# Attention layer in two stages: all projections by Strassen's scheme into DRAM, then scores to weighted values read back from DRAM, with the output projection in between

## The chip, the core and the metric

The kernel runs on one core of a Trainium2 chip. The metric is the device time of one execution in microseconds (us). The kernel before was run three times: median 2103.11 us, from 2101.34 to 2104.29. TensorE (PE) does matrix products and, with an identity matrix as one operand, transposes; its weight loads are listed apart (PEld). VectorE (DVE) and ScalarE (ACT) do elementwise work, GpSimd (POOL) does elementwise work and issues transfers, SyncE (SP) issues transfers. Each engine runs its own list of instructions in order.

## The reference

Two layers on x with 1024 tokens and 1024 channels, in float32. The first is a gated short convolution: a projection to 4 times 2048 columns, a causal convolution of width 3, gates, and a projection back to 1024. The second, which the change touches, is attention:

```python
h = rms_norm(x, attn_norm)
proj = h @ w_in                       # 1024 x (9*1024 + 1024)
for g, (window, dilation) in enumerate(((128, 1), (512, 4), (2048, 16))):
    q = rms_norm(proj_q[g], q_gain[g]); k = rms_norm(proj_k[g], k_gain[g])   # 16 heads of 64
    logits = q @ k.T / 8 + bias_g     # causal, every dilation-th token, 129 keys at most
    outs.append(softmax(logits) @ v);  lses.append(logsumexp(logits))
alpha = softmax(stack(lses), axis=0)  # weights of the three groups, by token and head
y = sum(alpha * outs) * silu(z)
x = x + y @ w_out
```

Of the 10240 columns of `proj`, 3072 each are q, k and v and 1024 are z.

## The kernel before

Activations lie transposed: 128 channels on the partitions, tokens along the free axis. A float32 product is made of three matmuls: each operand is split into a rounded high part (ACT) and the rest (DVE), and high times high, high times low and low times high are added up in PSUM. One such product covers 128 output rows, 128 contracted channels and 512 tokens.

There are four stages on PE.

*Conv input projections.* The first two of 16 column blocks (e) are plain; the other 14, two pairs each, go by Strassen's scheme: a pair of weight tiles of 128 columns by 1024 channels against both token halves needs seven block products of four contracted tiles, thus 7 x 4 x 3 = 84 matmuls (L398, L400, L401) where the plain scheme needs eight and 96. POOL adds and subtracts the weight halves (`mix`), ACT and DVE split them (L161, L162), ACT copies and DVE adds the products (L410). The weights of the next pair are prepared during this one.

*Conv output projection* (L544 to L546), 768 matmuls, for the two token halves one after the other. Its operand `yq` is read from DRAM and split. The result x1 goes to DRAM and, scaled and split, into `h1`.

*Attention projections with the attention in between.* The 80 weight tiles (q, k, v for each of 24 pairs of a head pair hp and a group g, z for each hp) are 80 x 48 = 3840 matmuls (L617 to L619). q and k get squared sums (L653, L654), one small matmul that adds and swaps them (L664), a reciprocal root (L76 to L80), a transpose that broadcasts it (L675), and a product (L682), which DVE does for q and POOL for k. v is scaled (L696) and transposed in two groups of four on PE (L705), z goes through silu. The attention of a unit (hp, g) is four steps for g = 0 and 1 and two for g = 2, thus 80 steps. A step has three parts: A, up to eight score matmuls (L759), then on DVE a maximum that also adds the bias (L767), on ACT an exponential (L770); B, up to eight transposes of the result (L780) and two copies out of PSUM by DVE or ACT in turn (L716); C, up to eight matmuls with the values (L791), then the copy of the sums `po`. After the third group of a head pair, `weights` works out the three groups' weights (L828 to L838) and sends them through DRAM (`fd`), from where they come back broadcast over partitions (`fb`, L844); D multiplies and adds (L853 to L856). What of the projections stands between two steps is set by a planner: a list of items with a cost each (0.645 for three matmuls), due times with `LEAD` and `LAST`, and `fill(to)`, which issues projection matmuls up to the due time; then C, B and A of earlier steps follow with high priority (lags 4 to 0). PE keeps the order that is written; on the other engines a scheduler sets it.

*Output projection.* Tiles 0 to 5 of the contraction (L941 to L943) start between the last steps; tiles 6 and 7 (L1014 to L1016) and the sums into `part` (L945, L1017) are the end. y goes through DRAM (`yd`) for tiles 0 to 5 and is split again (L907, L908).

## Time and profile before

The profiled execution took 2107.1 us, with a span of 2105.3 us; the mean granted clock of PE is 0.994 of full speed. Stage by stage (busy times are sums of the instructions in the window):

| window, us | what | length | PE busy | DVE busy | ACT busy | POOL busy |
|---|---|---|---|---|---|---|
| 101.0 to 641.0 | 28 Strassen pairs of the conv layer | 540.0 | 537.4 | 339.7 | 195.6 | 349.0 |
| 641.0 to 826.6 | conv output projection | 185.6 | 180.4 | 102.1 | 71.4 | 41.5 |
| 826.6 to 1975.0 | attention projections and attention | 1148.4 | 1131.9 | 611.9 | 476.6 | 159.6 |
| 1975.0 to 2105.3 | rest of the output projection | 130.3 | 111.3 | 60.0 | 32.8 | 15.8 |

A row of a grouped view (by line, or by form) names the line, engine, operation and tiles, then busy time, mean of one in ns, and the idle time of the engine just before, with what ended most of it. A matmul's mean is the length of its record, and records of PE overlap: the pitch, at which one follows the other, is window length over count.

### The profile page before, as it was taken

To read this page: it belongs to the slowest core of one execution; us is meant where nothing else is said; L and a number is where in the kernel's file an instruction comes from. 1 tells how busy PE (TensorE), PEld (TensorE's weight loads), DVE (VectorE), ACT (ScalarE), POOL (GpSimd) and SP (SyncE) were. 2 spreads that over 40 slices of the span, in tenths; PEclk is the share of its full clock that TensorE was granted. 3 is DMA by queue.
4 is the path that set the end of the run, shared out by engine and by line. 5 is a ranking of instruction groups with operands and counts; after the bars stand their busy time and mean duration, and the time that the engine had idled before them with its cause. 6 is when DMAs were issued, how large, how long until landed. Compare 5 with 4: busy or idle time off the path is not lost. (4 is left out here: it accounts for less than half of the span.)

```text
span 2105.3 us, 27817 instructions
## 1 busy us (share of the span) xinstructions
PE 2053.5 (98%) x10478; PEld 1653.8 (79%) x10478; DVE 1191.7 (57%) x2409; ACT 830.0 (39%) x1776; POOL 590.1 (28%) x568
## 2 busy tenths in 40 slices
PE   8999999999998999999999999999999999999897
PEld 6887788888886888877777777777777777777686
DVE  7866756666555554545644644645556546446544
ACT  6433333333333342243343444433433434443430
POOL 0466666666752222001201201102012012011020
PEclk9999999999999999999999999999999999999999
DMA  6245421122126553111211211212112112113142
GB/s 205 95 113 136 111 75 65 66 76 71 65 75 202 177 187 121 45 44 37 78 47 41 77 43 54 73 45 77 44 47 76 43 47 76 44 52 98 53 124 101
DMA packets 66071, 173.93 MB, mean 83 GB/s; under 512 B 9758, under 2 KB 10526, under 8 KB 65936
## 3 DMA queue, kind: packets, MB, share of 16 engines
q1 hardware_dynamic: 49248, 120.78, 18.0%
q0 software_dynamic: 16688, 51.37, 9.2%
q8 instruction: 82, 1.34, 0.3%
q14 instruction: 53, 0.43, 0.1%
HBM read 151.63 MB, written 28.87 MB: 86 GB/s over the span
## 5 line engine op out<-in xcount | busy, mean ns | idle before, releaser
L617 PE MATMUL pp<-h,whi 128*128 128x512 f32 x1280 | 513.6, 401 | 0.0
L619 PE MATMUL pp<-h,wlo 128*128 128x512 f32 x1280 | 499.7, 390 | 0.0
L618 PE MATMUL pp<-h,whi 128*128 128x512 f32 x1280 | 499.0, 390 | 0.0
L617 PEld LDWEIGHTS pp<-h,whi 128*128 128x128 f32 x1280 | 240.6, 188 | 67.5 <-issue 20.6
L69 DVE TENSOR_TENSOR wlo<-wraw,whi 128x1024 fp32r<-128x1024 f32 (+1 forms) x122 | 155.6, 1276 | 228.2 <-ACT whi L68 228.2
L619 PEld LDWEIGHTS pp<-h,wlo 128*128 128x128 f32 x1280 | 240.3, 188 | 51.6
L618 PEld LDWEIGHTS pp<-h,whi 128*128 128x128 f32 x1280 | 240.7, 188 | 45.4
L68 ACT ACTIVATE whi<-wraw 128x1024 fp32r<-128x1024 f32 (+1 forms) x122 | 127.4, 1044 | 307.2 <-PE pp L618 195.4
L770 ACT ACTIVATE xs<-xs,nl 128x128 f32<-128x128 f32 (+1 forms) x384 | 168.6, 440 | 110.6 <-DVE nl L767 110.4
L682 POOL TENSOR_TENSOR qk<-raw,tmp 128x512 f32<-128x512 f32 x48 | 62.5, 1303 | 415.7 <-DVE tmp L675 377.2
L398 PE MATMUL pp<-b,ws 128*128 128x512 f32 x448 | 174.8, 390 | 1.4 <-ACT f L406 1.4
L401 PE MATMUL pp<-b,ws 128*128 128x512 f32 x448 | 174.3, 389 | 0.0
L400 PE MATMUL pp<-b,ws 128*128 128x512 f32 x448 | 174.3, 389 | 0.0
L731 POOL DMA_DIRECT2D bt<-sk x48 | 26.8, 558 | 414.8 <-DVE nl L767 409.3
L654 DVE TRANSPOSE_TENSOR_REDUCE st<-tmp 128x16 f32<-128x512 f32 x96 | 67.9, 708 | 130.2 <-ACT tmp L653 130.0
L162 DVE TENSOR_TENSOR ws<-sr,ws 128x512 fp32r<-128x512 f32 x112 | 97.1, 876 | 69.6 <-ACT ws L161 67.7
L398 PE MATMUL pp<-t,ws 128*128 128x512 f32 x336 | 130.9, 390 | 1.2 <-ACT f L406 1.2
L400 PE MATMUL pp<-t,ws 128*128 128x512 f32 x336 | 130.7, 389 | 0.0
L401 PE MATMUL pp<-t,ws 128*128 128x512 f32 x336 | 130.7, 389 | 0.0
L162 DVE TENSOR_TENSOR ws<-wr,ws 128x512 fp32r<-128x512 f32 x100 | 107.1, 1074 | 39.5 <-ACT ws L161 38.4
L767 DVE CUSTOM_DVE_ANT_0 xs<-ps,bt 128x128 f32<-128x128 f32 (+1 forms) x384 | 111.9, 346 | 21.7 <-PE ps L759 21.5
L161 ACT ACTIVATE ws<-sr 128x512 fp32r<-128x512 f32 x112 | 70.2, 629 | 128.3 <-PE pp L401 85.6
(194 smaller groups left out, 3668.1 us busy)
## 6 DMA issues: line engine op xcount, KB each, us to landing
wr<-in_conv_w_in SPq DMA_DIRECT2D x128, 256.0 KB, 2.9
wraw<-in_wqk SPq DMA_DIRECT2D x48, 512.0 KB, 3.5
wraw<-in_conv_w_out SPq DMA_DIRECT2D x32, 512.0 KB, 4.2
wraw<-in_wv SPq DMA_DIRECT2D x24, 512.0 KB, 3.6
fb<-fd POOLq DMA_DIRECT2D x48, 256.0 KB, 4.3
f<-in_x SPq DMA_DIRECT2D x32, 256.0 KB, 5.3
ydc<-f POOLq DMA_DIRECT2D x32, 256.0 KB, 2.7
yr<-ydc SPq DMA_DIRECT2D x32, 256.0 KB, 4.0
```

What stands on the lines that cost most here:

```text
L68: nc.scalar.activation(hi[:, cs], raw[:, cs], AF.Copy)
L69: nc.vector.tensor_tensor(lo[:, cs], raw[:, cs], hi[:, cs].bitcast(F32), op=OP.subtract)
L161: nc.scalar.activation(t[:, 0], src, AF.Copy)
L162: nc.vector.tensor_tensor(t[:, 1], src, t[:, 0].bitcast(F32), op=OP.subtract)
L398: nc.tensor.matmul(ps, w[:, 0, ws], b[:, k, 0], start=new and k == 0, stop=False, skip_group_check=not new)
L400: nc.tensor.matmul(ps, w[:, 0, ws], b[:, k, 1], start=False, stop=False, skip_group_check=not new)
L401: nc.tensor.matmul(ps, w[:, 1, ws], b[:, k, 0], start=False, stop=end and k == 3, skip_group_check=not new)
L617: nc.tensor.matmul(ps, whi[:, ws], h1[:, kt, 0, cs], start=(kt == 0), stop=False)
L618: nc.tensor.matmul(ps, whi[:, ws], h1[:, kt, 1, cs], start=False, stop=False)
L619: nc.tensor.matmul(ps, wlo[:, ws], h1[:, kt, 0, cs], start=False, stop=(kt == KT - 1))
L767: nc.vector.tensor_tensor_reduce(out=x, in0=ps[s][:, x0:x0 + nk].rearrange("p a b -> p (a b)"), in1=u["bt"][s][:, bs], op0=OP.add, op1=OP. ...
L770: nc.scalar.activation(x, x, AF.Exp, bias=nm, scale=-1.0, accum_out=L)
```

## The change

The attention layer is cut in two.

1. *Blocks of the second layer's operand.* All tiles of the first stages come from one pool with seven slots of 16 KB (`blk`) and 12 + 3 tiles of 2 KB. The conv output projection runs in quarters of its contraction (`chunk(hf, dt, q)`); its first operand block is loaded in the last Strassen pair (`load_y(0, 0)`). While it runs, `row` makes the blocks that Strassen's scheme needs of h: B for the first token half, T1 and T2 (differences of blocks) from the second; `rest` makes T3, T4 and the last block after it, reading x1 back from DRAM.
2. *All 80 projection tiles as 40 Strassen pairs* (24 for q and k, 12 for v, 4 for z): 40 x 84 = 3360 matmuls in place of 3840. The seven products are PE work of lines L300 to L303 of the new kernel. `norm` of a pair stands two pairs later; all four products with the reciprocal root are on DVE now, with the gain in the same instruction. q and k go to DRAM (`qkd`) already in the order of their dilation, v transposed (`vd`; the transposes use one PSUM bank, `cst`), z after silu (`zd`). The statistics of the second token half and the two `spread` of them stand between the first pair's products.
3. *Then the 80 attention steps in a loop of their own*, without projections between them. A step's C stands three steps after its A, its B two (`LC`, `LB`), `weights` four, D eight (`LD`). The operands are loaded from DRAM six steps ahead, the bias three. `sp` has three PSUM banks in place of two, `opp` two in place of one; the copies of `po` are all on DVE.
4. *The output projection by rows of weights*: tiles 0 to 3 of the contraction as 16 groups of 12 matmuls, one in each of steps 49 to 64, tiles 4 and 5 as 16 groups of 6 in steps 69 to 84, tiles 6 and 7 at the end. y stays on chip (`y2`), split in D.

```diff
+        def block(tag=None):
+            return sl.tile([P, 4, 2, HALF], F32R, name=tag or "blk", tag="blk", bufs=7)
...
+            t = fp.tile([P, HALF], F32, name="f", tag="f", bufs=12)
...
+        def strassen(sources, pair, between, made):
+            w = [list(prepare(*sources[0]))[-1]]
+            made()
+            last = None
+            for n in range(len(sources)):
+                now = pair(n, w[n])
+                nxt = prepare(*sources[n + 1]) if n + 1 < len(sources) else iter(())
+                for at, (name, who) in enumerate(((1, now), (2, now), (4, last), (6, now), (5, now), (3, last), (7, now))):
+                    if who is not None:
+                        who[name]()
+                    between(n, at)
+                    got = next(nxt, None)
+                    if got is not None and len(w) == n + 1:
+                        w.append(got)
+                last = now
+            last[4]()
+            last[3]()
...
+                i = dt % 4
+                if hf == 0:
+                    if i == 0:
+                        B[dt // 4, 0] = block()
+                    parts_of(B[dt // 4, 0], i, x1, g2[:, dt:dt + 1])
+                elif dt < 4:
+                    if i == 0:
+                        T[1] = block()
+                    t = V1[i] = x1_tile(0, i)
+                    nc.vector.tensor_tensor(t, x1, t, op=OP.subtract)
+                    nc.scalar.activation(t, t, AF.Copy, scale=g2[:, i:i + 1])
+                    parts_of(T[1], i, t)
+                else:
+                    if i == 0:
+                        T[2] = xb.tile([P, 4, 2, HALF], F32R, name="xb", tag="xb")
+                    t = V1[i]
+                    nc.vector.scalar_tensor_tensor(t, x1, g2[:, dt:dt + 1], t, op0=OP.mult, op1=OP.subtract)
+                    parts_of(T[2], i, t)
...
+                if hf == 0:
+                    load_y(0, 0)
+                for dt in range(2):
+                    WO[dt, 0] = out_w(dt, 0)
+                for q in range(hf == 0, 4):
+                    load_y(hf, q)
+                for dt in range(2):
+                    WO[dt, 1] = out_w(dt, 1)
+                for q in range(4):
...
+                    if hf == 1 and dt == 2:
+                        stats(0, cst, sm)
+                    elif hf == 1 and dt == 3:
+                        spread(0, rtok, cst)
+                    elif hf == 1 and dt == 4:
+                        spread(0, ms2, cst)
...
+            units = [(hp, g) for hp in range(HP) for g in range(G)]
+            pairs = []
+            for m in range(12):
+                if m % 3 == 2:
+                    pairs.append(("z", 2 * (m // 3)))
+                pairs += [("qk",) + units[2 * m], ("qk",) + units[2 * m + 1], ("v", 2 * m)]
...
+                def norm():
+                    pst = cst.tile([P, HALF], F32, name="st", tag="st")
+                    nc.tensor.matmul(pst[:, :64], swap, u["st"].rearrange("p w c -> p (w c)"), start=True, stop=True)
...
+                    for hf in range(2):
+                        for which in range(2):
+                            raw = u[which, hf]
+                            rb = ftile()
+                            nc.vector.transpose(rb.rearrange("p (c q) -> p c q", q=32),
+                                                ri[:, which * 32 + hf * 16:which * 32 + (hf + 1) * 16, None]
+                                                .to_broadcast([P, 16, 32]))
+                            o = out_tile()
+                            nc.vector.scalar_tensor_tensor(o.rearrange("p (c s) -> p s c", c=c),
+                                                           raw.rearrange("p (s c) -> p s c", c=c),
+                                                           gain[:, g, which:which + 1],
+                                                           rb.rearrange("p (s c) -> p s c", c=c),
+                                                           op0=OP.mult, op1=OP.mult)
+                            nc.gpsimd.dma_start(qkd[hp, g, which].rearrange("p (c s) -> p c s", c=c)
...
+                def turn(col, q):
+                    hp, g = units[p[1] + col]
+                    vt = spare()[:, col * S:col * S + S]
+                    pv = cst.tile([P, 4, P], F32, name="st", tag="st")
+                    for i in range(4):
+                        nc.tensor.transpose(pv[:, i], blk(vt, g, 4 * q + i), ident)
+                    o = ftile()
+                    if q:
+                        nc.vector.tensor_copy(o, pv.rearrange("p a b -> p (a b)"))
+                    else:
+                        nc.scalar.activation(o, pv.rearrange("p a b -> p (a b)"), AF.Copy)
+                    nc.gpsimd.dma_start(vd[hp, g, q], o)
...
+                if kind == "qk":
+                    due[n + 2, 0] = [norm]
+                elif kind == "v":
+                    for i in range(4):
+                        due[n + 2, i + 1] = [lambda i=i: turn(i // 2, i % 2)]
...
+            def between(n, at):
+                if n == 0 and at == 1:
+                    stats(1, cst, sm)
+                elif n == 0 and at == 3:
+                    spread(1, rtok, cst)
+                elif n == 0 and at == 4:
+                    spread(1, ms2, cst)
+                for f in due.pop((n, at), ()):
...
+            def rest():
+                for n in (3, 4):
+                    T[n] = block()
+                    for i in range(4):
+                        kt = i + 4 * (n == 4)
+                        t = x1_tile(0, kt)
+                        if n == 3:
+                            nc.vector.scalar_tensor_tensor(t, t, ng2[:, kt:kt + 1], V1[i], op0=OP.mult, op1=OP.add)
+                        else:
+                            nc.vector.scalar_tensor_tensor(t, t, g2[:, kt:kt + 1], V1[i], op0=OP.mult, op1=OP.subtract)
+                        parts_of(T[n], i, t)
+                B[1, 1] = block()
+                for i in range(4):
+                    parts_of(B[1, 1], i, x1_tile(1, i + 4), g2[:, i + 4:i + 5])
...
+            strassen([sources(p) for p in pairs], pair, between, rest)
...
+        def loads(hp, g):
+            QK[hp, g] = [ap.tile([P, S], F32, name="qk", tag="qk", bufs=5) for _ in range(2)]
+            for i in range(2):
+                nc.sync.dma_start(QK[hp, g][i], qkd[hp, g, i])
+            VS[hp, g] = ap.tile([P, 8, P], F32, name="V", tag="V", bufs=3)
+            for q in range(2):
+                nc.sync.dma_start(VS[hp, g][:, 4 * q:4 * q + 4].rearrange("p a b -> p (a b)"), vd[hp, g, q])
...
-                if hp < 6:
-                    nc.gpsimd.dma_start(yd[hp], SZ[hp])
-                else:
-                    split_y(hp, SZ[hp])
+                y2[hp] = ap.tile([P, 2, S], F32R, name="y2", tag="y2", bufs=5)
+                nc.scalar.activation(y2[hp][:, 0], SZ[hp], AF.Copy)
+                nc.vector.tensor_tensor(y2[hp][:, 1], SZ[hp], y2[hp][:, 0].bitcast(F32), op=OP.subtract)
...
-                    steps.append(make(js, not steps))
+                    st = make(js, not steps)
+                    steps.append(dict(zip((0, LB, LC), st)))
                     if g == 2 and q == 1:
-                        steps[-1] += [lambda: None, D]
+                        steps[-1][LC + 1] = weights
...
+        def some(kts, dt, hf):
+            if dt not in part:
+                part[dt] = ap.tile([P, S], F32, name="part", tag="part", bufs=KT)
+                nc.sync.dma_start(part[dt], x1d[dt])
+            ps = pp1.tile([P, HALF], F32, name="pd", tag="pd")
+            dense(ps, kts, dt, hf, True, True)
+            nc.vector.tensor_tensor(part[dt][:, half(hf)], ps, part[dt][:, half(hf)], op=OP.add)
...
+            begins.setdefault(max(0, k - 6), []).append(lambda un=un: loads(*un))
+            begins.setdefault(max(0, k - 3), []).append(prefetch)
...
+        def put(kts, k):
+            begins.setdefault(k - 2, []).append(lambda: rows(kts))
+            for n, (dt, hf) in enumerate(tiles):
+                extra.setdefault(k + n, []).append(lambda dt=dt, hf=hf: some(kts, dt, hf))
+        put((0, 1, 2, 3), at[4, 0][0] + LD + 1)
+        put((4, 5), at[6, 0][0] + LD + 1)
+        end = len(steps) + LD
+        k = 0
+        while k < end or any(x >= k for x in extra):
...
+            for lag in (LD, LC + 1, LC, LB, 0):
+                if 0 <= k - lag < len(steps) and lag in steps[k - lag]:
+                    steps[k - lag][lag]()
+                if lag == LC:
+                    for f in extra.get(k, ()):
+                        f()
+            if k == end - 4:
+                rows((6, 7))
+            k += 1
```

Three places show how the instructions stand. PE, in the middle of the attention of one unit, before: `h` is the operand of the projections, `qk`, `xs`, `pts` and `V` are those of parts A, B and C.

```order
L617 MATMUL pp<-h_5694,whi 128x512
L618 MATMUL pp<-h_5694,whi 128x512
L619 MATMUL pp<-h_5694,wlo 128x512
L791 MATMUL po<-pts,V 64x128 x8
L780 MATMUL pt<-ident,xs 128x128 x6
L759 MATMUL ps<-qk 128x256 x4
L617 MATMUL pp<-h_5694,whi 128x512
L618 MATMUL pp<-h_5694,whi 128x512
L619 MATMUL pp<-h_5694,wlo 128x512
```

The same place now:

```order
L876 MATMUL pt<-ident,xs 128x128 x8
L855 MATMUL ps<-qk 128x128 x2
L855 MATMUL ps<-qk 128x256 x2
L887 MATMUL po<-pts,V 64x128 x8
L876 MATMUL pt<-ident,xs 128x128 x8
L855 MATMUL ps<-qk 128x256 x4
L887 MATMUL po<-pts,V 64x128 x8
L876 MATMUL pt<-ident,xs 128x128 x6
```

Between the parts of one step and those of the next there stands no matmul of 512 columns any more.

DVE, at the start of the projections of the attention layer, where the reciprocal root of the second token half (`rtok`, of `ms`) is made. Before, its first instructions:

```order
L107 TENSOR_SCALAR ms_79<-pp 128x4
L76 TENSOR_SCALAR rtok<-ms_79 128x4
L78 TENSOR_TENSOR rtt<-rtok 128x4
L79 SCALAR_TENSOR_TENSOR rtt<-rtt,ms_79 128x4
L80 SCALAR_TENSOR_TENSOR rtok<-rtt,rtok 128x4
```

Now, from the first instruction of its last three rounds on (`rtt`; `blk` is a block of h, `ws` a piece of a weight; L69 to L71 are what L78 to L80 were):

```order
L69 TENSOR_TENSOR rtt<-rtok 128x4
L520 TENSOR_TENSOR blk<-f,blk 128x512
L523 SCALAR_TENSOR_TENSOR blk<-f,attn_norm,blk 128x512
L520 TENSOR_TENSOR blk<-f,blk 128x512
L660 TENSOR_REDUCE st<-f 128x16
L70 SCALAR_TENSOR_TENSOR rtt<-rtt,ms_77 128x4
L166 TENSOR_TENSOR ws<-sr,ws 128x512
L71 SCALAR_TENSOR_TENSOR rtok<-rtt,rtok 128x4
```

Five of 512 columns stand between three small ones that were neighbours, and twelve more between the first of the chain (L99, which was L107) and L69; two more rounds without any in between end it. PE has its transposes of `rtok` (L107 of the new kernel) after the third product of the first pair.

DVE, from the weights of the groups (`fo`) to the first use of what comes back (`fb`). Before:

```order
L838 TENSOR_TENSOR fo<-f,mx 128x8x6
L654 TENSOR_REDUCE st<-tmp 128x16
L69 TENSOR_TENSOR wlo<-wraw,whi 128x1024
L654 TENSOR_REDUCE st<-tmp 128x16
L853 TENSOR_TENSOR o<-o,fb 128x512 x2
```

Now, around the place where L853, now L948, stands (`xs,nl<-ps,bt` is the maximum with the bias, part A):

```order
L863 ISA xs,nl<-ps,bt 128x256
L863 ISA nl 128x1
L948 TENSOR_TENSOR o<-o,fb 128x512 x2
L812 COPY pts<-pt 128x512
L863 ISA xs,nl<-ps,bt 128x128
```

Between `fo` (L838, now L933) and L948 there now stand, in place of the projections' three instructions, twelve such maxima, one copy of `po` and two of `pt`, all of later attention steps; behind L948 wait a copy of `pt` and the next step's maxima.

720 lines of the change are left out of this document (290 added, 430 removed).

## The prediction

> **What bounds the kernel now.** I read the page's busy line first, then windows by stage, then groups by form.
>
> ```profile
> PE 2053.5 (98%) x10478; PEld 1653.8 (79%) x10478; DVE 1191.7 (57%) x2409; ACT 830.0 (39%) x1776; POOL 590.1 (28%) x568
> ```
>
> PE is busy 98% of the span. The windows (core 0; length, then busy time and instructions of PE, PEld, DVE, ACT, POOL, then granted clock, DMA share, GB/s) say where it isn't:
>
> ```profile
> 101.00:641.00 540.00, 537.42 (x2359) 441.17 (x2358) 339.74 (x388) 195.55 (x333) 348.99 (x272) 1.00 0.29 84
> 641.00:826.60 185.60, 180.35 (x786) 147.74 (x786) 102.14 (x110) 71.42 (x97) 41.50 (x51) 0.98 0.56 183
> 826.60:1975.00 1148.40, 1131.93 (x6374) 902.49 (x6374) 611.90 (x1650) 476.60 (x1176) 159.61 (x194) 1.00 0.20 57
> 1975.00:2105.30 130.30, 111.31 (x556) 86.85 (x555) 60.02 (x133) 32.84 (x82) 15.78 (x22) 0.93 0.33 106
> ...
> 300.00:400.00 100.00, 100.00 (x443) 82.79 (x442) 61.80 (x71) 36.47 (x63) 67.64 (x51) 1.00 0.21 69
> ```
>
> The last row is the price of a matmul of 512 columns: 443 in 100 us of full PE, 0.2257 us each. The first row is that of a Strassen pair, DVE, ACT and POOL work included: 540.0 / 28 = 19.29 us, where 84 x 0.2257 = 18.96. The third is the stage that the change cuts in two: DVE has only 53% there, and every wait of the attention is covered by projection matmuls. So time goes down with the matmuls only as long as something else covers those waits. These rows, picked from the groups by form, carry the prices (line, engine, operation, tiles, shape, count | busy us, mean ns | idle before):
>
> ```profile
> L791 PE MATMUL po<-pts,V 128*64 128x128 f32 x1120 | 78.8, 280 | 0.0
> L780 PE MATMUL pt<-ident,xs 128*128 128x128 f32 x560 | 78.7, 281 | 0.0
> L759 PE MATMUL ps<-qk 64*128 64x256 f32 x352 | 51.3, 391 | 0.0
> L759 PE MATMUL ps<-qk 64*128 64x128 f32 x416 | 38.3, 299 | 0.0
> L705 PE MATMUL pp<-ident,vt 128*128 128x128 f32 x192 | 30.6, 281 | 13.8 <-DVE V L716 9.3 <-ACT tmp L653 4.5
> L664 PE MATMUL pp<-st,swap 128*128 128x64 f32 x48 | 8.1, 251 | 2.7 <-DVE st L654 2.7
> L162 DVE TENSOR_TENSOR ws<-wr,ws 128x512 fp32r<-128x512 f32 x100 | 107.1, 1074 | 39.5 <-ACT ws L161 38.4
> L162 DVE TENSOR_TENSOR ws<-sr,ws 128x512 fp32r<-128x512 f32 x112 | 97.1, 876 | 69.6 <-ACT ws L161 67.7 <-POOL f L293 0.5
> L410 DVE TENSOR_TENSOR f<-pp,f 128x512 f32<-128x512 f32 x84 | 57.8, 688 | 58.4 <-PE pp L401 58.1 <-issue 0.3
> L654 DVE TRANSPOSE_TENSOR_REDUCE st<-tmp 128x16 f32<-128x512 f32 x96 | 67.9, 708 | 130.2 <-ACT tmp L653 130.0
> L675 DVE STREAM_TRANSPOSE tmp<-ri 128x512 f32<-128x512 f32 x96 | 62.2, 685 | 0.5
> L682 DVE TENSOR_TENSOR qk<-raw,tmp 128x512 f32<-128x512 f32 x48 | 54.2, 1157 | 0.0
> L682 POOL TENSOR_TENSOR qk<-raw,tmp 128x512 f32<-128x512 f32 x48 | 62.5, 1303 | 415.7 <-DVE tmp L675 377.2 <-DVE y L908 33.9 <-ACT qk L907 2.6
> L716 DVE COPY pts<-pt 128x512 f32<-128x512 f32 x40 | 27.8, 694 | 55.9 <-PE pt L780 55.9
> L716 DVE COPY pts<-pt 128x384 f32<-128x384 f32 x40 | 22.2, 554 | 21.1 <-PE pt L780 21.1
> L716 DVE COPY o<-po 128x512 f32<-128x512 f32 x16 | 14.4, 897 | 5.3 <-PE po L791 5.3
> L716 DVE COPY o<-po 128x256 f32<-128x256 f32 x16 | 10.3, 646 | 48.8 <-PE po L791 48.8
> L854 DVE TENSOR_TENSOR o<-o 128x512 f32<-128x512 f32 x16 | 10.8, 680 | 0.0
> ```
>
> **Removed.** 3840 - 3360 = 480 matmuls: 480 x 0.2257 = 108.3 us of full PE. That is the whole gain there can be, but for idle time that goes. The sum below asks how much comes back as idle time, stage by stage.
>
> **Stage 1 (to 641.0).** Same products, same order: 641.
>
> **Conv output projection.** 768 x 0.2257 = 173.3 us where 185.6 are spent. Part of the rest is the boundary, where PE waits for the first operand block:
>
> ```profile
> PE pp L544 <- ACT yq L516: 4.5, 1, 4.5
> ```
>
> (4.5 us, once.) With the first block loaded in the last Strassen pair, that wait and the slow clock behind it go. More DVE and ACT work stands there (T1, T2), but DVE was at 102 of 186 us. I take 175; bounds 173 and 186, the old length.
>
> **Start of the projections.** PE's transposes of `rtok` stand after the first pair's third product. The root they need stands on DVE between the large instructions of `rest`, about 28 of 0.7 us (as in rows L410 and L654) and 11 small ones of 0.2, by its order from the last sum of x1 on: 21.4 us after the last conv matmul, and 1 more to reach PE. PE meanwhile has three products, 36 x 0.2257 = 8.1 us. Idle: 14. After a gap of that size the clock is low for some time:
>
> ```profile
> 1991.67 0.80 PE L941 MATMUL pp<-y,whi 128*128 128x512 f32 x1 [3.45 <-ACT y L907]
> ...
> 1992.00:1994.00 2.00, 2.00 (x5) 1.32 (x5) 0.94 (x2) 0.13 (x1) 0.54 (x1) 0.50 0.02 4
> ```
>
> After a wait of 3.45 us the clock was 0.50, and five matmuls took the 2.00 us in which nine go at 0.2257. Some 7 us like that would cost 3. I take 17; bounds 2 (the order on DVE hurts nobody) and 25.
>
> **The 40 pairs.** 40 x 19.29 = 771, and what the conv pairs had not: V's transposes (30.6, row L705) and the swaps (8.1, row L664), 810 together. DVE for a q/k pair: splits of eight weight pieces of 0.876 to 1.074, 6.7 with a share on ACT; three sums 2.1; four square sums 2.8; the root 2.4; four transposes 2.7; four products 1.157 each 4.6; about 21 us, over PE's 19.3. A v pair has about 11 and a z pair 9.5: 24 x 21 + 12 x 10.8 + 4 x 9.5 = 672 of 810. POOL now gives 1.3 us products away (row L682 POOL) but issues four transfers a pair. Two q/k pairs follow each other, then a v pair gives time back, and weights are made a pair ahead; I take 10 us for what leaks: 820. Bounds 810 and 843 (below).
>
> **Between the stages.** After the last v pair come a product with the root, four groups of transposes through one PSUM bank (5.2), the bias loads behind them on POOL, and the first step before PE has something to do. 14 us; bounds 8 and 20.
>
> **The 80 steps.** On PE a step is (78.8 + 78.7 + 51.3 + 38.3) / 80 = 3.1 us. DVE has the maxima, which the window of that line alone gives (length, DVE busy, count, clock), and ACT the exponentials, in the second row:
>
> ```profile
> 0.00:2105.30 2105.30, 112.73 (x768) 0.99 0.28 83
> 0.00:2105.30 2105.30, 198.23 (x784) 0.99 0.28 83
> ```
>
> To DVE's 112.7 come 50.0 for half the copies of `pt`, 49.4 for all copies of `po` (32 x 0.897 + 32 x 0.646), 54.4 in D (80 x 0.68), 22 for the sums of `part` and 10 for the split of y: 299 us, 3.7 a step, with ACT at 2.5 and more. So PE, which had 98%, waits for DVE at every step. And the weights' way through DRAM, which projections covered, is on DVE's path:
>
> ```profile
> 1310.74 0.25 DVE L838 TENSOR_TENSOR fo<-f,mx 128x48 f32<-128x48 f32 x1
> ...
> 1320.99 1.56 DVE L853 TENSOR_TENSOR o<-o,fb 128x512 f32<-128x512 f32 x2 [1.56 <-DMA fb<-fd]
> ```
>
> From `fo` to `fb` in place: 10.2 us. Between them DVE now has 12 maxima, a copy of `po` and two of `pt`, about 6.1 us of work. It stands 4.1 us at the first product, and behind it wait copies and maxima that PE's next B and A need. Ten steps make a head pair: 0.4 a step. The third group's transfer is issued only after POOL has read the first, as its row in the same list shows; below it the transfer's (KB, median us to landing) and that of the bias loads:
>
> ```profile
> 1321.69 1.08 POOL L844 DMA_DIRECT2D fb<-fd  x2 [0.29 <-POOL o L853]
> ```
>
> ```profile
> fb<-fd POOLq DMA_DIRECT2D x48, 256.0 KB, 4.3
> ...
> L731 POOL DMA_DIRECT2D bt<-sk x48 | 26.8, 558 | 414.8 <-DVE nl L767 409.3
> ```
>
> That gives a second stall: two products on POOL at 1.3, 1.1 to issue and 4.3 for the transfer are 8 us, against 4.6 of other work on DVE and 1.4 of its own, thus 2 us or 0.2 a step. Bounds 3.7 and 4.3; I take 4.1, since PE's buffers (three of `ps`, eight of `xs`) cover a short stall more easily than a long one. Steps 0 to 48: 201. In steps 49 to 64 come 12 x 0.2257 = 2.7 us of output projection, which fill the waits: 3.1 + 2.7 + 0.2 = 6.0, 96 us. Steps 65 to 79: 15 x 4.1, and 0.7 for each of 11 groups of six matmuls: 69.
>
> **The tail.** B and C of the last steps 5; the weights' ten small instructions and the way to `fb` 16; D with its split 8; 78 matmuls of tiles 6 and 7, 17.6; the last sum and turn-round 3; and the output transfer, by the end of the chain of waits:
>
> ```profile
> 2101.24 0.69 DVE V L1017
> ```
>
> 4.1 from there to the span's end. 54 together; bounds 45 and 65.
>
> **Sum.** 641 + 175 + 17 + 820 + 14 + 201 + 96 + 69 + 54 = 2087, against a span of 2105.3: 18 less. The profiled execution took 2107.1 with what lies around its span; so 2089 for an execution like it, and 2085 against the median of 2103.11. Of 108 us, some 90 come back as idle time.
>
> **Rivals.**
>
> *A. The waits overlap.* `ps` has three banks, `xs` eight buffers, B and C stand two and three steps behind A, so DVE's 3.7 is only an average with D in it: a step goes at 3.3, with D's work and the fb wait absorbed by those buffers. The stage and its tail then save 54: 2087 - 54 = 2033, 2031 by the median. For it: row L780 waits for nothing (0.0) at a lag of one to two steps. Against: DVE's own sum is above 3.3.
>
> *B. DVE's queue blocks (the side of slower).* The place is L948 and the second stall at it, of the third group's `fb`. POOL's list also holds the bias loads (48, 0.56 to issue each), which now stand within 80 short steps, and they wait for maxima on DVE, as row L731 did before (409 us of waits): POOL stands there, the third `fb` is issued late, DVE stands at L948, and the next maxima with it. If that makes the 8 us 15 and the stalls 13 in place of 4 a head pair, a step takes 5.0: 64 steps x 0.9 = 58, so 2145, by the median 2143. It decides once the stalls exceed 7 us a head pair, where the 18 us gained are gone. For it: two engines that wait for each other in order. Against: the bias is loaded three steps ahead.
>
> *C. DVE bounds the projections.* Ten pairs (six q/k, three v, one z) are 168 us of DVE against 202 of PE. If DVE's instructions take a quarter longer, as the two rows of L162 of one shape differ (1074 to 876), ten take 210 and all 843; with the 10 that leak 2087 + 33 = 2120, by the median 2118. For it: 21 over 19.3 in 24 of 40 pairs. Against: in the conv stage POOL was as busy (349 of 540), and DVE's rows include that.
>
> *D. The clock drops in the attention stage.* If the gap of each step counts as the 3 us gaps above did, PE runs at half speed: 6.2 a step in 49 and in 15 steps, 64 x 2.1 = 134, so 2221, by the median 2219. For it: the clock of 0.93 in the last stage, where PE has gaps. Against: a step's gaps are 1 us or less, and two waits of that length (row: total us, times, longest) left the clock of the window at 101 to 641 at 1.00:
>
> ```profile
> PE pp L398 <- ACT f L406: 2.6, 2, 1.4
> ```
>
> The Trainium skill speaks for it ("TensorE: Matmul & The Clock Gate", section "A second HAM failure mode: psum-queue depth-cycling"): PE that idles briefly between groups of matmuls, while cycling through PSUM banks, was seen to swing between half and full clock, and to lose throughput between bursts. By that page this rival would be the likely one; the row of 0.93 goes some of the way with it.
>
> **How the numbers follow.** Forecast 0.46, A 0.25, B 0.13, C 0.08, D 0.08. A difference of 0.2%, 4 us, is what a measurement can tell from none. The forecast's own range adds up the squares of its terms' bounds (2, 15, 10, 6, 26 and 9 below; 11, 8, 23, 6, 13 and 11 above): 33 and 32, thus 2052 to 2117. The range of 2028 to 2143 takes in A, B and C and leaves out D and the far ends. Faster: A's 0.25 and 0.33 of the forecast's 0.46, together 0.58; within 0.2%: 0.05 of the forecast and 0.02 of C, 0.07; slower: 0.08 of the forecast, B, the rest of C, and D, 0.35.
>
> **What would show it.** Right: L300 of the new kernel at 3360 matmuls in three lines with a window of 820; one PE wait of 14 us at L107; PE near 75% in the 49 steps, waiting for DVE's maxima and copies, clock at 1.00; waits of DVE for `fb` of 4 to 6 us in all, for each of eight head pairs. Wrong: steps at 3.3 or at 5 and more, a clock of 0.5 there, a projection window over 830, or a PE idle at the cut between stages beyond 20.

## The result, and the profile after

The changed kernel takes 2164.8 us, median of 4 runs (2162.81 to 2169.72); the kernel before took 2103.02 beside it (4 runs). The ratio is 1.0298, 95% interval 1.0277 to 1.0318: slower by 3%. The forecast was 2085 in a range of 2028 to 2143, so both the sign and the range were missed. The profiled execution's span is 2161.3 us, 56 more than before.

The page's busy line, and the windows of the stages (length, then busy time and instructions of PE, PEld, DVE, ACT, POOL, then granted clock, DMA share, GB/s):

```profile
PE 1981.3 (92%) x9998; PEld 1603.6 (74%) x9998; DVE 1511.5 (70%) x2832; ACT 893.4 (41%) x2004; POOL 900.4 (42%) x857
```

```profile
851.00:1662.00 811.00, 795.53 (x3566) 652.35 (x3567) 653.53 (x981) 318.91 (x554) 374.72 (x352) 0.99 0.31 100
1662.00:1692.00 30.00, 5.07 (x26) 3.59 (x26) 16.13 (x26) 4.36 (x5) 9.11 (x13) 0.59 0.64 204
1692.00:1900.00 208.00, 148.32 (x1312) 111.30 (x1310) 131.54 (x563) 119.70 (x467) 48.48 (x74) 0.85 0.59 181
```

PE has 480 records fewer and 72 us less busy time, and its share fell from 98% to 92%. The projections run at 98% of PE (first row): their matmuls are gone for good. The 30 us behind them hold 5 us of PE, and in the 208 us of attention that follow PE is busy 71% at a clock of 0.85. What PE waited for (engine and line, releaser: us in total, times, longest), and the two waits of DVE that stand behind it:

```profile
PE po L887 <- DVE pts L812: 75.1, 23, 8.5
...
PE ps L855 <- DMA qk<-qkd: 17.3, 2, 16.5
...
PE po L887 <- DVE o L900: 15.5, 4, 3.9
```

```profile
DVE mx L923 <- DMA ml<-nld: 52.3, 8, 9.4
...
DVE o L948 <- DMA fb<-fd: 30.2, 12, 4.2
```

`ml` is what `weights` reads: the maxima and sums of groups 0 and 1, which come back from DRAM (`nld`) in the token order of group 2. It is the first half of the weights' way, before `fo`. One head pair shows the chain. POOL stores `nl` and, when that has landed, issues the load of `ml`; DVE stands at it; PE stands at a copy behind it; and the matmuls after the wait have records twice as long (start, length, engine, line, count, in brackets the idle time before it and its releaser):

```profile
1766.42 1.51 POOL L912 DMA_DIRECT2D nld<-nl  x2
1773.79 0.56 POOL L871 DMA_DIRECT2D ml<-nld  x1 [5.86 <-DMA nld<-nl]
```

```profile
1779.97 0.18 DVE L923 TENSOR_TENSOR mx<-ml 128x16 f32<-128x16 f32 x1 [8.36 <-DMA ml<-nld]
1780.06 1.05 DVE L902 COPY o<-po 128x256 f32<-128x256 f32 x2
1780.95 0.68 DVE L812 COPY pts<-pt 128x512 f32<-128x512 f32 x1
```

```profile
1781.69 1.97 PE L887 MATMUL po<-pts,V 128*64 128x128 f32 x16 [8.50 <-DVE pts L812]
1783.59 1.97 PE L876 MATMUL pt<-ident,xs 128*128 128x128 f32 x8
1785.49 1.94 PE L855 MATMUL ps<-qk 64*128 64x256 f32 x8
1787.36 1.09 PE L887 MATMUL po<-pts,V 128*64 128x128 f32 x16
```

The part of the way that the prediction counted, from `fo` to `fb`, costs DVE 30 us; the part that it left out costs 52.

The forecast's terms against the trace (us; a stage ends where the next one's first matmul starts, at 652.7, 835.7, 1662.1, 1691.3 and 1922.9; the tail starts after the last score at 2106.2):

| term | forecast | measured | difference |
|---|---|---|---|
| stage 1 | 641 | 652.7 | +11.7 |
| conv output projection | 175 | 183.0 | +8.0 |
| start of the projections and 40 pairs | 17 + 820 | 826.4 | -10.6 |
| between the stages | 14 | 29.2 | +15.2 |
| steps 0 to 48 | 201 | 231.6 | +30.6 |
| steps 49 to 79 | 96 + 69 | 183.3 | +18.3 |
| tail | 54 | 55.1 | +1.1 |
| span | 2087 | 2161.3 | +74.3 |

### The profile page after: what moved, and what is told of

It is laid out like the page before. It is cut to its first block, busy times and chain, and to the rows that moved or that the text cites. A ratio compares the mean times of both kernels' runs of the same rounds, so it can differ in the third digit from the quotient of the medians.

```text
span 2161.3 us, 28871 instructions
## 1 busy us (share of the span) xinstructions
PE 1981.3 (92%) x9998; PEld 1603.6 (74%) x9998; DVE 1511.5 (70%) x2832; ACT 893.4 (41%) x2004; POOL 900.4 (42%) x857
## 5 line engine op out<-in xcount | busy, mean ns | idle before, releaser
L300 PE MATMUL pp<-blk,ws 128*128 128x512 f32 x1744 | 688.3, 395 | 10.5 <-ACT f L308 10.4
L303 PE MATMUL pp<-blk,ws 128*128 128x512 f32 x1744 | 681.1, 391 | 0.0
L302 PE MATMUL pp<-blk,ws 128*128 128x512 f32 x1744 | 680.6, 390 | 0.0
L300 PEld LDWEIGHTS pp<-blk,ws 128*128 128x128 f32 x1744 | 328.9, 189 | 85.0 <-ACT f L308 16.6
L303 PEld LDWEIGHTS pp<-blk,ws 128*128 128x128 f32 x1744 | 328.3, 188 | 69.8
L302 PEld LDWEIGHTS pp<-blk,ws 128*128 128x128 f32 x1744 | 328.8, 189 | 66.3
L166 DVE TENSOR_TENSOR ws<-wr,ws 128x512 fp32r<-128x512 f32 x284 | 274.0, 965 | 142.2 <-ACT ws L165 140.8
L165 ACT ACTIVATE ws<-wr 128x512 fp32r<-128x512 f32 x284 | 178.6, 630 | 393.8 <-PE pp L303 225.8
L166 DVE TENSOR_TENSOR ws<-sr,ws 128x512 fp32r<-128x512 f32 x272 | 228.9, 848 | 93.6 <-ACT ws L165 92.1
L165 ACT ACTIVATE ws<-sr 128x512 fp32r<-128x512 f32 x272 | 169.6, 629 | 299.8 <-PE pp L303 237.0
L275 POOL TENSOR_TENSOR sr<-wr 128x512 f32<-128x512 f32 x136 | 184.4, 1356 | 248.4 <-DMA wr<-in_wqk 60.0
L312 DVE TENSOR_TENSOR f<-pp,f 128x512 f32<-128x512 f32 x204 | 139.7, 685 | 89.6 <-PE pp L303 83.5
L887 PE MATMUL po<-pts,V 128*64 128x128 f32 x1120 | 95.4, 308 | 94.4 <-DVE pts L812 75.1
L308 ACT ACTIVATE f<-pp 128x512 f32<-128x512 f32 x228 | 132.5, 581 | 27.7 <-PE pp L303 14.5
L275 POOL TENSOR_TENSOR sr<-sr,wr 128x512 f32<-128x512 f32 x68 | 102.7, 1510 | 4.6
```

The costliest lines, as they stand in the source:

```text
L165: nc.scalar.activation(t[:, 0], src, AF.Copy)
L166: nc.vector.tensor_tensor(t[:, 1], src, t[:, 0].bitcast(F32), op=OP.subtract)
L275: nc.gpsimd.tensor_tensor(t, x, y, op=op)
L300: nc.tensor.matmul(ps, w[:, 0, ws], b[:, k, 0], start=new and k == 0, stop=False, skip_group_check=not new)
L302: nc.tensor.matmul(ps, w[:, 0, ws], b[:, k, 1], start=False, stop=False, skip_group_check=not new)
L303: nc.tensor.matmul(ps, w[:, 1, ws], b[:, k, 0], start=False, stop=end and k == 3, skip_group_check=not new)
```

## Experiments

Theory 1, from this profile: DVE stands in its list at two transfers per head pair (`ml`, `fb`), PE stands behind it, and each such stop of PE is followed by microseconds of longer records, as in the rows above. Its rival: DVE's own 3.7 us a step, with PE's 3.1, sets the pace, and the waits lie in slack. Theory 2: the 16.5 us at the first score are SP's list. Theory 3: PE's waits for `o` are D holding the buffers.

The kernel before ran beside each set: 2101.01 us beside the runs without the way through DRAM, without the loads, and with DVE's order as written; 2106.5 beside those with one more buffer, with the first loads moved, and with the weights held back; 2105.68 beside the next two; 2103.93 (11 runs) beside the last and beside the one without `ml`. All but one of the kernels below were run once, with a profile. The executions of the one that was run six times lie up to 8 us apart, so a difference of that size between two single runs is open. The edits are abridged: `...` stands for code that is not shown.

### The weights' way through DRAM left out

```diff
-    nc.gpsimd.dma_start(u["ml"], nld[hp]...)      # ml: a constant tile
-    nc.gpsimd.dma_start(fb[hs], fd[hp, w, s]...)  # fb: a constant tile
```

> Left out: the weights' way through DRAM. The lines that load ml and the three fb are gone, and the weights and D read constant tiles instead, so the merge of the groups is not computed; every instruction of DVE, ACT and PE stays. Theory 1 (DVE stands in its list waiting for ml, 52 us in eight times, and for fb, 30 us in twelve, and PE behind it, with a slow clock after each): steps 0 to 48 go from 5.0 us to about 3.8, the tail loses some 15, time about 2085. Rival (DVE's and PE's own work sets the pace, the waits only sit where slack is): time not below 2140.

Measured: 2077.2 us, 88 below the changed kernel and 24 below the kernel before. Steps 0 to 48 took 174.5 us (1696.0 to 1870.5), 3.56 each. PE's wait for the copies; then one window, from 1692 to 1940, of this kernel and of the changed one:

```profile
PE po L890 <- DVE pts L816: 29.2, 27, 2.6
```

```profile
1692.00:1940.00 248.00, 219.86 (x1966) 166.96 (x1967) 201.35 (x817) 167.74 (x653) 53.83 (x71) 0.95 0.55 183
```

```profile
1692.00:1940.00 248.00, 174.38 (x1501) 131.53 (x1500) 154.66 (x655) 137.06 (x538) 56.98 (x86) 0.83 0.57 175
```

Every instruction of DVE, ACT and PE was still there. The rival falls: with the same work on DVE and PE a step takes 3.56 us and not the changed kernel's 4.73. The clock rises from 0.83 to 0.95 with the same instructions on PE, so it follows the stops.

One thing moved with the waits. The scheduler sets DVE's order by when it takes the data to be there, and a constant tile is always there: the first product of D now stands ahead of the first `fo`.

```profile
1728.28 1.30 DVE L948 TENSOR_TENSOR o<-o,fbc 128x512 f32<-128x512 f32 x2
...
1733.75 0.24 DVE L936 TENSOR_TENSOR fo<-f,mx 128x48 f32<-128x48 f32 x1
```

So the run takes away the waits and also frees the places of `weights` and D in DVE's list; it gives what both are worth together.

### Only the load of ml left out

```diff
-    nc.gpsimd.dma_start(u["ml"], nld[hp]...)      # ml: a constant tile
```

> Left out: the load of ml alone; the weights read a constant tile, so the groups' shares are wrong; fd and fb go through DRAM as before. Without both ways the kernel took 2077 us, 88 less than the changed kernel. If the two waits add up by their length on DVE (ml 52 us, fb 30 us), ml is worth 56 of the 88: 2109. If the wait for fb is the one that decides, since it drags D and the copies into o behind it: 2130 to 2150. If ml alone decides: below 2090.

Measured: 2139.58 us, 25 below the changed kernel. DVE's wait for `ml`, 52 us, went, and its wait for `fb` grew by 26:

```profile
DVE o L949 <- DMA fb<-fd: 55.8, 11, 9.3
...
DVE wlo L60 <- ACT whi L59: 12.6, 4, 6.7
```

So the two waits do not add by their lengths: with the first gone, DVE comes to the second earlier and stands there longer (9.8 us on PE where it had 8.5). The time lies in the range of the second expectation. `ml` alone is worth 25 of the 88 us; the other 63 came when `fb` went too, and a run without `fb` alone was not made.

### No loads of q, k and V after the second unit

```diff
+    if (hp, g) < (0, 2):  # load
+    else: QK[hp, g], VS[hp, g] = QK[0, g % 2], VS[0, g % 2]
```

> Left out: the loads of q, k and V of all units after the second; the later units work on the first two units' tiles. Theory 1a (ml lands in 5.4 us and nld in 5.8 instead of 2 because the operand loads fill the DMA engines): both land in 2 to 3 us, the wait of DVE for ml falls from 52 us to 15 or less, time about 2120. Rival (the landing times come from POOL's queue or from the shape of these transfers): landing and waits as they were, time 2155 to 2165, but for the 16 us at the first score.

Measured: 2130.71 us. The landing times of `ml` (us from issue, least, median, most) in the kernel before, the changed one and this one, and DVE's wait in this one:

```profile
DMA to landing us min/median/max: 1.9/2.1/3.2
```

```profile
DMA to landing us min/median/max: 1.9/5.4/6.2
```

```profile
DMA to landing us min/median/max: 2.0/2.1/2.9
```

```profile
DVE o L951 <- DMA fb<-fd: 30.1, 12, 3.6
...
DVE mx L926 <- DMA ml<-nld: 24.1, 8, 5.1
```

A transfer of 32 KB took 2.1 us where the projections covered it, and 5.4 where the operands of the next units load at the same time. That is new in this kernel, since q, k, V and z now go through DRAM, and without those loads about half of the wait for `ml` goes (52 to 24 us). The time fell by 34 us, and not all of that need be `ml`: the larger bias loads land in 2.5 us (median) in place of 6.1 as well. The wait for `fb` did not change. The landing of `ml` came out as theory 1a expected; the wait (15 or less) and the time (about 2120) did not come down as far.

### DVE's order as written

```diff
-    tc.manual_schedule(engines={PE})
+    tc.manual_schedule(engines={PE, DVE})
```

> Nothing left out: DVE's order in the attention stage is as written (like PE's) instead of the scheduler's, with the same lags (weights 4 steps after A, D 8) and one more buffer for o. Theory 1: the weights stand about where they stood, DVE waits for ml as before, time 2150 to 2180. Rival (the scheduler's order on DVE is itself the loss): below 2130.

> Nothing left out: as the run before it, with the weights 7 steps after A in place of 4 and D 12 in place of 8 (five buffers for o, six for xs). Theory 1: three steps are 10 us or more, so the wait for ml goes, and most of that for fb; steps at 3.8 to 4.1, time 2085 to 2110. Rival (DVE's and PE's own work sets the pace): above 2140.

Measured: 2182.62 and 2186.54 us, both slower. `ml` is not among DVE's waits in either run, also not in the first, where the weights stand four steps behind A as before and the expectation had DVE wait for it as before. The gain did not come: PE's wait for the copies, 75.1 us in the changed kernel, rose. In the first run it was

```profile
PE po L887 <- DVE pts L812: 126.7, 18, 27.7
```

As written D is one block of ten instructions of 0.69 us. DVE stands at the bias and at `fb` ahead of it, and the copies wait behind the block. DVE and then PE in the run with the later weights:

```profile
1804.95 0.29 DVE L863 CUSTOM_DVE_ANT_0 xs<-ps,bt 128x128 f32<-128x128 f32 x1 [3.20 <-DMA bt<-sk]
...
1811.26 0.69 DVE L948 TENSOR_TENSOR o<-o,fb 128x512 f32<-128x512 f32 x1 [1.84 <-DMA fb<-fd]
...
1820.82 0.68 DVE L812 COPY pts<-pt 128x512 f32<-128x512 f32 x1
```

```profile
1821.56 1.97 PE L887 MATMUL po<-pts,V 128*64 128x128 f32 x16 [14.78 <-DVE pts L812]
```

As written, the four splits of the output projection's weights are one block as well: in this run DVE waited for three of them in a row for 14 us, D came right behind, and PE stood 30.2 us. So the order was changed in more than the place of two waits, and the two runs do not decide on theory 1. The first came out just above its range and without the wait that the range was built on; the second is a miss.

### One more buffer for o

```diff
-    O[hp, g] = ap.tile(..., tag="o", bufs=3)
+    O[hp, g] = ap.tile(..., tag="o", bufs=4)
```

> Nothing left out. Four buffers for o in place of three. Theory 3 (PE's 15.5 us of waits for the first copy into o, four times, is that copy's wait for D to leave a buffer): this wait goes, and with it its slow clock, time 2140 to 2155. Rival (DVE stands at fb there anyway, and the copy behind it): PE's wait moves to the copies of pt, time 2160 to 2166.

Measured: 2140.71 us, 24 less, for one more buffer. With three buffers, the first copy of the next head pair's `po` waits until D has read a buffer, and D waits for `fb`; DVE in the changed kernel shows it in between (`L950` is D's sum that reads it, `L900` the copy):

```profile
1757.89 0.69 DVE L950 TENSOR_TENSOR o<-o 128x512 f32<-128x512 f32 x1
1758.49 1.28 DVE L900 COPY o<-po 128x512 f32<-128x512 f32 x2
```

PE's wait for `o` is not in its list in this run, and 73.5 us of waits for the copies of `pt` stay. Theory 3 holds for the time (within its 2140 to 2155); what the fourth buffer gave is more than the 15.5 us of that wait, and DVE's wait for `ml` fell from 52 to 31 us with it, while that for `fb` rose from 30 to 38, for a reason that no run separates.

### The first loads

```diff
-    raw = wp.tile([P, 1024], F32, tag="wraw", bufs=1)
+    raw = ap.tile([P, 1024], F32, tag="wraw", bufs=1)
```

> Nothing left out. The buffer through which the output projection's weights are loaded is taken from the attention stage's pool, so that their four loads stand behind the first q, k and V loads in SP's list. Theory 2 (PE's 16.5 us at the first score is SP standing at those four loads until 1684.7): the first score comes 6 to 10 us earlier, since the stores of q and k end at about 1678, and the time is 2155 to 2160. Rival (the stores or the place in memory keep the load back): first score at 1691 as before, time 2164.

In the changed kernel SP's list, before and at the first load of q and k (start, and for a group the time from first to last), and PE's wait:

```profile
1644.99 39.72 SPq L58 DMA_DIRECT2D wraw<-in_wo  x4
1684.87 0.82 SPq L798 DMA_DIRECT2D qk<-qkd  x2
```

```profile
1691.33 4.12 PE L855 MATMUL ps<-qk 64*128 64x128 f32 x16 [16.54 <-DMA qk<-qkd]
```

The scheduler put four loads of the output projection's weights, needed at step 49, ahead of the first q and k; they share one buffer, so each waits for ACT and DVE to split the one before. With them behind, the first score came at 1679.7 us, 11.6 earlier: theory 2 holds for the wait. The time was 2171.39 us, not less, and steps 0 to 48 took 248.0 us in place of 231.6. The four splits now stand between the first steps. PE's waits for `ps` behind DVE rose to 21.9 us, but two of them, 8.5 and 7.2 us, come later, at 1834 and 1889, and each ends a microsecond after DVE has stood at `ml`; the first of those:

```profile
1832.96 0.17 DVE L923 TENSOR_TENSOR mx<-ml 128x16 f32<-128x16 f32 x1 [11.03 <-DMA ml<-nld]
```

So the gain was given back, in part at the waits of theory 1; how much of it the splits cost is not separated.

### Weights and D held back in the scheduler's order

In the changed kernel the scheduler, and not the place in the program, sets where `weights` and D stand in DVE's list, as the run without the way through DRAM showed. So a number that a later step's exponential writes is made an operand (times zero):

```diff
+    z = sm.tile([P, 1], F32, tag="z"); nc.vector.tensor_scalar(z, recent["L"], 0.0, add, ...)
-    nc.vector.tensor_tensor(mx, ml0, ml1, op=OP.min)
+    nc.vector.scalar_tensor_tensor(mx, ml0, late(0.0), ml1, op0=OP.add, op1=OP.min)
```

and the same in D with 1.0. `weights` stands six steps behind A and D eleven (four and eight before), with five buffers for `o` in place of three and six for `xs` in place of eight.

> Nothing left out. The scheduler keeps DVE's order, but the first weights instruction and the products with fb also read a sum that a later step's exponential wrote (times zero), so they can't stand earlier in DVE's list than 5 and 10 steps behind; five buffers for o, six for xs. Theory 1 (the places of the waits in DVE's list cost the time, not the transfers and not the order of the rest): the wait for ml and for fb go to under 10 us each, PE's waits for the copies of pt fall from 75 us to 30 as in the run without the way through DRAM, time 2080 to 2105. Rival (any order in which DVE waits less only moves the wait to the o or bias buffers, as the order as written did): above 2140.

Measured: 2131.29 us, 33.5 less than the changed kernel, between the two expectations. One more buffer for `o` alone had given 24, and this run has two more, so what the tie itself is worth is not separated. The wait for `ml` is gone; `fb` still costs 27.5 us, of whose transfers the third still waits for a buffer, and PE waits behind D for a copy of `po`:

```profile
PE po L894 <- DVE o L912: 30.2, 3, 11.4
```

> Nothing left out. The tied weights and D, and the loads moved behind q, k and V, together. If the two causes are separate, their gains add up: 6 to 10 us below the tied run, 2072 to 2098, below the kernel before. If the tied run's loads collide with the moved ones: no gain over it.

Measured: 2138.94 us. No gain over the tied run, as when the loads were moved alone; the first expectation, 2072 to 2098, is a miss.

### What the waits still hung on, one after the other

Three buffers for `fb`, six for `o`, the output projection in pairs of contraction tiles from step 31 on (so three buffers for `y2` pay for them), and the split of its weights held back like the others:

```diff
-    put((0, 1, 2, 3), at[4, 0][0] + LD + 1)
+    put((0, 1), at[2, 0][0] + LD + 1); put((2, 3), at[4, 0][0] + LD + 1)
-    nc.scalar.activation(hi, raw, AF.Copy)
+    nc.scalar.activation(hi, raw, AF.Copy, scale=late(1.0))
```

> Nothing left out. The tied weights and D as before, and what the tied run still waited for is taken away: three buffers for fb (all three groups load at once), six for o (the copy of po never waits for D), the output projection's tiles in pairs from step 31 (so three buffers for y2 do), and the split of its weights tied to a late step too, so that one of its loads and not four stands ahead of q, k and V. Theory 1 (waits on DVE's list and what they drag): first score 10 us earlier, wait for fb under 10 us, PE's waits for copies under 45 us, time 2075 to 2100, below the kernel before. Rival (the stage is bound by DVE's and PE's work with those transfers beside it): 2125 to 2140 as the tied run.

Measured: 2112.36 us; first score at 1678.4, `fb` 10.0 us, PE's waits for copies 36.6. The waits went about as expected (`fb` was to be under 10) and the time came out 12 above the top of its range.

The bias loads in SP's queue:

```diff
-    nc.gpsimd.dma_start(b0[:, :n], sk...)
+    nc.sync.dma_start(b0[:, :n], sk...)
```

> Nothing left out. As the run before it, and the bias loads go through SP's queue in place of POOL's, where they stood up to 23 us waiting for DVE with the weights' transfers behind them. If POOL's list is what delays fb and ml: 5 to 15 us below the run before it. If the bias loads only waited in slack: within 4 us of it, or above it, since SP's loads of q and k would then wait behind them.

Measured: 2105.27 us, 7 less, level with the kernel before beside it (2105.68). This one difference rests on one execution each. It was expected to come by way of `fb` and `ml`, and did not: DVE's wait for `fb` rose from 10.0 to 12.6 us, and that for `ml` was gone in the run before already. What fell is DVE's own wait for the bias, in the run before and in this one:

```profile
DVE xs L869 <- DMA bt<-sk: 14.3, 5, 5.5
```

```profile
DVE xs L869 <- DMA bt<-sk: 2.4, 1, 2.4
```

Then D 13 steps behind, the output projection's groups two steps later and its last ones two a step, and the last head pair's weights not held back:

```diff
-    LB, LC, LW, LD = 2, 3, 6, 11
+    LB, LC, LW, LD = 2, 3, 6, 13
-    put((0, 1), at[2, 0][0] + LD + 1)  # and the other two
+    put((0, 1), at[2, 0][0] + LD + 3)
```

> Nothing left out. As the run with the bias loads in SP's queue, and three places where it still waited: D stands 13 steps behind (its products waited 12.6 us for fb), the groups of the output projection start two steps later after D (PE waited 19.4 us in three places for the split of y) and the last of them go two to a step once no steps are left, and the last head pair's weights are not held back. Theory 1: the waits for fb and for the split of y go under 8 us each, and with the slow clock behind them 10 to 20 us: time 2085 to 2095, faster than the kernel before. Rival (what is left is DVE's and PE's own work): within 5 us of 2105.

Measured in five rounds: 2089.27 us, median of 6 runs (2084.55 to 2092.78), against 2103.93 for the kernel before, 11 runs: ratio 0.9924, 95% interval 0.9907 to 0.9942. That is 0.8% less than the kernel before and 3.5% less than the changed kernel, with all of the computation, and inside the range of theory 1. PE's wait for the split of y is gone, and `fb` came near the 8 us. DVE's and PE's waits, and the window that stood at 0.83:

```profile
DVE o L957 <- DMA fb<-fd: 8.6, 3, 4.1
```

```profile
PE po L894 <- DVE pts L818: 22.1, 14, 5.9
```

```profile
1692.00:1940.00 248.00, 220.08 (x2002) 167.41 (x1999) 210.54 (x838) 171.04 (x657) 50.26 (x69) 0.96 0.67 191
```

PE is as busy in these 248 us as in the run without the way through DRAM (220 us), at about the same clock (0.96 and 0.95). This run differs from the changed kernel in many places at once, so it shows that the waits can be taken away with the computation kept, and not what each place is worth.

## Why the prediction was wrong

**What bounds the kernel, and what is removed** was right. 480 matmuls went, and the profile says where the time that they had covered came out. The prediction's own sentence, that time falls with the matmuls only while something else covers the waits, is what happened; the sum under it was too small.

**The step that failed is the price of a step of attention**, 4.1 us with bounds of 3.7 and 4.3. Steps 0 to 48 took 231.6 / 49 = 4.73, and the 80 steps were 49 us over their forecast. The sum's own terms, 3.7 + 0.4 + 0.2, already make the upper bound, so nothing was left for a stop that they had not named. The terms themselves were not too small: DVE's work (3.7, of which 22 us in all are sums of `part` that only come behind step 48) stands against 3.56 in the run without the waits, and `fb`, at 4 to 6 us a head pair, against 30.2 / 8 = 3.8. What failed is what was left out. Three things were not in the sum. First, the weights' way through DRAM was counted from `fo` to `fb`, and its first half, `nl` to DRAM and back as `ml`, was not; it is the longer wait of the two (52.3 against 30.2 us on DVE). In the kernel before it cost DVE 5.7 us, with a landing time of 2.1 us; the rows of a wait that is covered do not show what it costs uncovered. Second, D holds the three buffers of `o`, and the next head pair's copies wait for it; one more buffer was worth 24 us. Third, the clock: the stops of PE in the head pair shown were followed by records of up to double length, which the prediction priced at the start of the projections (3 us) and not here. By an estimate from the two windows, 0.17 of PE's 174 busy us at 0.83 are 30 us, against 11 at 0.95. The three overlap, since a stop brings the slow records behind it; no run gives the share of each.

**The rivals.** Rival B named the right mechanism, two engines that wait in order and DVE's list standing at a transfer, and the right sign; its place (the third `fb` and the bias loads in POOL's list) was only a part: the stops at `fb` are 3.8 us a head pair, with those at `ml` 82.5 / 8 = 10.3, where the rival had 13 at `fb` alone, and the bias loads in SP's list gave 7 us in a later kernel. Its price, 2143 us, was 22 us short. The chance of 0.13 was too small for what the sum itself said: the first stall per head pair was in the forecast, and its own bounds were drawn as if no other could join it. Rival A, that waits overlap at 3.3 us a step, is near to what a kernel without those waits does (3.56). Rival D, half clock through the whole stage, did not happen: where PE's gaps were below 1 us the clock stayed at 1.00, as in this window of the changed kernel, and it fell behind the long stops:

```profile
1710.00:1720.00 10.00, 9.24 (x104) 7.02 (x100) 7.08 (x39) 7.69 (x34) 2.58 (x4) 1.00 1.02 385
```

The section of the Trainium skill's "TensorE: Matmul & The Clock Gate" that was cited for rival D, on brief idles between groups, does not fit this window. The one before it there, "HAM oscillation — how this bites in real kernels", sets the limit at idle gaps of some 3.4 us. The gaps of 8.5 us here lie above it and those of under 1 us below, as it says, but in between the trace does not keep to it: after 2.63 us, at 743, the granted clock was 0.50 (743 to 749), and after 2.06 us, at 263, it was 1.00. Rival C did not happen.

**The projections** came out 10 us better than forecast: 826.4 us against 837 with the start. Two q/k pairs in a row did not make PE wait for DVE, though DVE was busy 81% (653.5 of 811). At the start PE waited 7.8 us for a copy behind the large instructions and 4.5 for the root, 12.3 in all and 1.2 for the squares, close to the 14 forecast, with the place shared between two lines:

```profile
PE pp L300 <- ACT f L308: 8.5, 2, 7.8
```

```profile
PE st L107 <- DVE rtok L71: 4.5, 1, 4.5
```

**Between the stages** 14 us were forecast and 29.2 measured. The prediction named the loads in POOL's list there and none in SP's, where q and k stood behind four loads for a later use; with those moved, the first score came 11.6 us earlier.

**Stage 1** was put down as unchanged and took 11.7 us more; one wait of PE of 4.9 us for ACT's copy of a product, at 218, with records of 0.63 us behind it, is part of that; the pool of 2 KB tiles has 12 in place of 15 slots there, but no run tried whether that is the cause. In all thirteen profiled executions of kernels with the new first stages the stage ended late, between 650.7 and 657.7 us. **The conv output projection** has no wait at its start any more, as forecast, and still took 183.0 us: 2.6 less than the 185.6 before, where 10.6 were forecast. A wait like it, of 2.63 us, came back at the first block of the second token half, again with the slow clock behind it (0.50 from 743 to 749):

```profile
743.04 0.80 PE L550 MATMUL pp<-blk,ws 128*128 128x512 f32 x1 [2.63 <-ACT blk L519]
```

**The tail** was right (55.1 against 54).

## What to carry to other kernels

Work that fills an engine at 98% is also the cover of every wait beside it: before it is taken out, each round trip that other engines make (here store, load, compute, store, load) must be followed from end to end with its own rows, the covered half too, and priced as if nothing covered it. A wait that goes alone can lengthen the next one in the same list, as `ml` did with `fb`; the run that took away both at once showed what there was to win, and it is a good one to make first. Then give each waiting instruction a place that is late enough, and the buffers that such a place needs; try the buffers alone too, since one of them gave 24 us here.

## What was not expected of the hardware

A small transfer's landing time depends on what loads at the same moment: 32 KB (`ml`, median) in 2.1 us in the kernel before, 5.4 beside the loads of the next units, 2.1 again without them, and 2.3 in the first run with DVE's order as written, which keeps those loads. And small DVE instructions cost more in the new projection stage than in the old one: the root's steps of 64 columns took 0.22 us before and 0.49 now, with POOL busier beside them, its issuing of transfers included (375 us of 811, where the old stage had 160 of 1148); that POOL is the cause was not tried. The Trainium skill has a rule that would fit ("SBUF — State Buffer", section "SBUF: two separate sides"): DVE with two operands in SBUF and POOL share one pair of ports, and the one that comes second waits for the other's whole instruction; no run here separates it. The group before, and a group of the same shape and operation in the new stage:

```profile
L79 DVE SCALAR_TENSOR_TENSOR rit<-rit,ag 128x64 f32<-128x64 f32 x72 | 16.2, 224 | 1.7
```

```profile
L70 DVE SCALAR_TENSOR_TENSOR rit<-rit,ag 128x64 f32<-128x64 f32 x69 | 33.7, 488 | 1.6
```
